# Six instead of two feature tiles of a feed-forward block in plain matrix products, and the token sums of the seven-product form as background steps

## The chip, the core and the metric

The kernel is one program on one core of a Trainium2 chip. The metric is the device time of one execution in microseconds, the median of three runs. The engines of the core are called by the short names of the profile: PE multiplies matrices, DVE and ACT work elementwise and reach both memories of the chip, POOL works elementwise on one of them, and SP issues the transfers from the chip's main memory (its queue is SPq). PEld is the loading of PE's stationary operand.

## The reference

The reference computes one transformer block with a convolution and an mLSTM branch, then two more layers with attention. Only one part of it is touched here, the first feed-forward block, where s is 512 tokens, d is 1024 and f is 2816:

```
h = rms_norm(x, norm_ffn_g[l]) * (1.0 + sc2) + sh2
gt, up = jnp.split(jnp.einsum("bsd,df->bsf", h, w_ffn_up[l]), 2, axis=-1)
x = x + g2 * jnp.einsum("bsf,fd->bsd", jax.nn.silu(gt) * up, w_ffn_down[l])
```

sc2, sh2 and g2 come from a modulation vector, `mod = silu(c) @ w_ada + b_ada`, of which each of six sections has 1024 numbers. All is float32.

## The kernel before

Tokens lie along the columns of a tile (512), features along its 128 partitions. To keep float32 accuracy every operand is split into a rounded part and a rest ("hi" and "lo": a cast on ACT, then a subtraction on DVE or POOL), and each product is three matmuls, hi·hi, hi·lo and lo·hi (`mm3`, lines 368 to 371, which therefore carry nearly all matmuls of the profile).

The weights come in half units, 128x512 numbers, with `unit` (line 342): a transfer into one of four buffers "st" (L347), the cast to "wh" on ACT (L348), the rest "wl" on DVE (L351). After each half unit, `pull` runs steps of the background list `bg`, here one step for every second half unit.

The first feed-forward block (`ffn1`, line 1118) has 22 feature tiles of 128; each stands for two column tiles of w_up, one of the gate and one of the value. They are worked on in groups of 8, 8 and 6. After each group `tmat` multiplies by the rows of w_down that belong to it: eight output tiles, each added to x with a factor of the modulation vector (`add`, L1134).

Within the first group the first two feature tiles are done by `seven_head`: four column tiles side by side, eight steps over the depth, twelve 512-column matmuls in a step, or 24 of 256 columns where the tokens' operand was split in two halves of tokens. All other feature tiles go in pairs through `seven`, a form with seven half-size products in place of eight (it multiplies the 2x2 blocks of weights and tokens; sums and differences of weight blocks are made on DVE and POOL before the product, and those of the results after it). One pair takes 14 splits (`parts`: cast L1077, rest L1078), 168 matmuls of 256 columns, six sums of weight blocks (L1099 to L1101, L1113) and seven sums of results (L1103 to L1115).

The tokens' side is made once by `seven_x` (line 986), before `seven_head`: for each of four pairs of depth tiles the normalised token tiles h1 and h2 (L1157, L1159), their own splits (L999, L1000), and two tiles of block sums, ta on DVE and tb on POOL (L1005 to L1008), with their splits. The sums serve only the products called t1 to t4 in `seven`.

Two other pieces of work are issued while `seven_head` runs: `mid` (the rest of a memory projection, L1321 and L1328, and the tables of sines and cosines for the rotary embedding, `rope_tables`, lines 556 to 585, some thirty small DVE instructions) and, as background steps, the eight steps of `ada_ops(5)`: each loads two tiles of w_ada (L599) and multiplies and sums them on DVE (L601), and gives one column of the factors that `add` of w_down needs.

The order within each engine's queue is not written by hand. A scheduler takes the instructions by their place in the program, gives out buffers, and reckons with a model of durations which instruction is ready first. Each engine runs its queue strictly in that order. Buffers of a name ("q", "pt", "hs", "t", "wh") are a fixed number, and an instruction that needs a new one waits until an old one is free.

Of the kernel before, what the change touches and what calls it, by code (L numbers as in the profile page):

```python
# [8 lines left out]
ALU = mybir.AluOpType  # L9
# [3 lines left out]
P = 128  # L13
# [10 lines left out]
UNIT = 1024  # L24
FF_GROUPS = (8, 8, 6)
FIRST = 6
LOWEST = -3.4e38
# [198 lines left out]
class Net:  # L226
# [760 lines left out]
    def seven_x(self, hs):  # L987

        nc = self.nc
        m = S // 2
        pieces = [None] * KD
        ops = {n: [] for n in ("11", "21", "22", "t1", "t2", "t3", "t4")}
        todo = []

        def split(hi, lo, src, eng=nc.vector):
            nc.scalar.copy(hi, src)  # L999
            eng.tensor_tensor(out=lo, in0=src, in1=hi.bitcast(F32), op=ALU.subtract)  # L1000

        def sums(k, h1, h2):
            ta, tb = self.t(), self.t()
            l, r = slice(0, m), slice(m, S)
            nc.vector.tensor_sub(ta[:, l], h1[:, r], h1[:, l])  # L1005
            nc.gpsimd.tensor_tensor(out=tb[:, l], in0=h2[:, r], in1=h1[:, r], op=ALU.add)
            nc.vector.tensor_add(ta[:, r], h2[:, r], ta[:, l])
            nc.gpsimd.tensor_tensor(out=tb[:, r], in0=h2[:, l], in1=ta[:, r], op=ALU.subtract)  # L1008
            ah, al = self.two("hs")
            split(ah, al, ta)  # L1010
            bh, bl = self.two("hs" if k < 2 else "pt")
            split(bh, bl, tb, nc.gpsimd)
            for n, hi, lo, c in (("t1", ah, al, l), ("t2", ah, al, r), ("t3", bh, bl, l),
                                 ("t4", bh, bl, r)):
                ops[n].append((hi[:, c], lo[:, c]))

        for k in range(KD // 2):
            h1, h2 = hs(k), hs(k + 4)
            got = []
            for i in range(2):  # L1020
                z = self.slot("q" if i else "hs", dt=F32R)
                hi, lo = z[:, 0:m], z[:, m:S]
                split(hi, lo, h1[:, i * m:(i + 1) * m])
                got.append((slice(i * m, (i + 1) * m), hi, lo))
            pieces[k] = got
            ops["11"].append(got[0][1:])
            hi, lo = self.two("hs")
            split(hi, lo, h2)
            pieces[k + 4] = [(slice(0, S), hi, lo)]
            ops["21"].append((hi[:, 0:m], lo[:, 0:m]))  # L1030
            ops["22"].append((hi[:, m:S], lo[:, m:S]))
            todo.append((k, h1, h2))
            if k:
                sums(*todo.pop(0))
        sums(*todo.pop(0))
        return pieces, ops

    def seven_head(self, name, pieces, done, mid):
# [11 lines left out]
        for n in range(4):  # L1050
            done(n, pts[n])

    def seven(self, name, tiles, x, done):
# [64 lines left out]
    def ffn1(self):  # L1118
# [36 lines left out]
        def hs(k):  # L1155
            h = self.t()
            nc.vector.scalar_tensor_tensor(out=h, in0=self.x[k], scalar=self.aff[:, 8 + k:9 + k],  # L1157
# [3 lines left out]
            return h  # L1161
        pieces, x = self.seven_x(hs)

        def mid():
            self.run_all(mem)
            self.rope_tables()
        self.bg.append(self.ada_ops(5, "q"))
        self.bg_rate = 0.5
        f0 = 0
        for n in FF_GROUPS:  # L1170
            act = []
            if not f0:
                self.seven_head("w_up", pieces, lambda t, pt: up(t, pt, act), (None, mid))
            for f in range(f0 + 2 * (f0 == 0), f0 + n, 2):
                self.seven("w_up", (f, f + 1), x, lambda *z: up2(*z, act))
            self.tmat("w_down", f0, n, KD, act, add)
            f0 += n
# [686 lines left out]
```

## Time and profile before

| | us |
|---|---|
| runs shown | 2238.39, 2234.23, 2239.53 (median 2238.39) |
| profiled execution | 2234.19, its span 2232.5 |
| PE busy | 2151.7 (96% of the span) |
| DVE busy | 1495.4 (67%) |
| ACT busy | 1045.7 (47%) |
| POOL busy | 705.7 (32%) |

Busy time of PE is modelled with overlap, so PE can be shown as busy and yet run at half its clock: the granted clock has a column of its own (PEclk, 1.00 is full). The first feed-forward block's products begin at 550.4 us in the span, its first group ends at 709.7, the second at 835 and the third at 927.

### The profile page before, as it was taken

How to read it: one execution, taken by the hardware profiler on the slowest of the kernel's cores; microseconds unless marked ns; L12 is line 12 of the kernel's file. 1: busy time of each engine (PE TensorE's matmuls, PEld its weight loads, DVE VectorE, ACT ScalarE, POOL GpSimd, SP SyncE). 2: the span in 40 equal slices, each digit the busy share in tenths (PEclk: the TensorE clock that was granted, in tenths of full speed). 3: DMA queues.
4: the chain of work that ended last, by engine and by line, in shares of the span. 5: the costliest groups of instructions: out<-in, count | busy, mean ns of one | idle time of the engine just before them, and what ended most of it. 6: DMA issues, size and time to landing. Idle time of an engine off the chain costs nothing.

```text
span 2232.5 us, 30831 instructions
## 1 busy us (share of the span) xinstructions
PE 2151.7 (96%) x10756; PEld 1776.9 (80%) x10756; DVE 1495.4 (67%) x2823; ACT 1045.7 (47%) x1971; POOL 705.7 (32%) x630
## 2 busy tenths in 40 slices
PE   6999999999789999999989999999999999999998
PEld 4887778888688989877778888888887778888886
DVE  8889989445985968759975654545556665545354
ACT  4555466645443534645464432323555645323233
POOL 3554454553462716343441210101133321101010
PEclk9999999999899999999999999999999999999999
DMA  7344443233432332321211333322321112232232
GB/s 265 111 135 133 137 132 102 76 103 103 151 95 95 95 113 82 104 76 43 71 46 64 96 95 94 94 95 94 118 86 54 32 48 90 94 95 93 94 95 88
DMA packets 120544, 217.04 MB, mean 97 GB/s; under 512 B 13762, under 2 KB 18114, under 8 KB 120388
## 3 DMA queue, kind: packets, MB, share of 16 engines
q1 hardware_dynamic: 120388, 215.08, 30.3%
q8 instruction: 84, 1.38, 0.3%
q14 instruction: 72, 0.59, 0.1%
HBM read 212.93 MB, written 2.10 MB: 96 GB/s over the span
## 4 chain that ended last, share of the span: by engine, by line
PE 74%; DVE 9%; issue 2%; ACT 1%; POOL 1%; DMA 1%; SPq 0%; DVEq 0%; ACTq 0%; POOLq 0%
PE ps L369 24%; PE ps L370 24%; PE ps L371 24%; PE ps L503 2%; DVE bias L1610 1%; DVE bias L1572 1%; DVE m L1609 1%; POOL q L1078 1%; DVE big L361 0%; DVE q L601 0%; DMA q<-in_w_up_dram 0%; DVE rope L1281 0%; DVE x L1486 0%; DVE pt L1101 0%; DVE wl L1078 0%
## 5 line engine op out<-in xcount | busy, mean ns | idle before, releaser
L348 ACT CAST wh<-st 128x512 fp32r<-128x512 f32 (+1 forms) x618 | 378.3, 616 | 671.2 <-PE ps L370 417.6
L369 PE MATMUL ps<-hs,wh 128*128 128x512 f32 (+1 forms) x1720 | 653.5, 384 | 24.9 <-ACT wh L1077 11.4
L371 PE MATMUL ps<-hs,wl 128*128 128x512 f32 (+1 forms) x1720 | 652.9, 380 | 7.5 <-DVE wl L1078 5.0
L370 PE MATMUL ps<-hs,wh 128*128 128x512 f32 (+1 forms) x1720 | 654.5, 381 | 2.5 <-DVE hs L628 2.5
L351 DVE TENSOR_TENSOR wl<-st,wh 128x512 fp32r<-128x512 f32 x408 | 298.0, 732 | 206.1 <-ACT wh L348 201.7
L369 PEld LDWEIGHTS ps<-hs,wh 128*128 128x128 f32 x1720 | 326.2, 190 | 97.6 <-ACT wh L1077 12.9
L351 POOL TENSOR_TENSOR wl<-st,wh 128x512 fp32r<-128x512 f32 (+1 forms) x210 | 285.4, 1366 | 357.6 <-ACT wh L348 328.1
L371 PEld LDWEIGHTS ps<-hs,wl 128*128 128x128 f32 x1720 | 326.1, 190 | 75.8 <-DVE wl L1078 5.6
L370 PEld LDWEIGHTS ps<-hs,wh 128*128 128x128 f32 x1720 | 326.6, 190 | 69.6 <-DVE hs L628 3.8
L1212 POOL TENSOR_TENSOR t<-t,t 128x512 f32<-128x512 f32 x44 | 69.2, 1576 | 602.7 <-DVE t L1211 533.6
L643 DVE SCALAR_TENSOR_TENSOR big<-ps,vec,big 128x511 f32<-128x511 f32 (+28 forms) x240 | 164.9, 720 | 3.5 <-ACT big L640 3.5
L370 PE MATMUL ps<-big,wh 128*128 128x512 f32 x400 | 156.9, 394 | 0.0
L369 PE MATMUL ps<-big,wh 128*128 128x512 f32 x400 | 156.1, 394 | 0.0
L371 PE MATMUL ps<-big,wl 128*128 128x512 f32 x400 | 156.1, 394 | 0.0
L361 DVE TENSOR_TENSOR big<-t,big 128x512 fp32r<-128x512 f32 (+1 forms) x106 | 74.1, 717 | 80.9 <-ACT big L360 80.6
L369 PE MATMUL ps<-wh,hs 128*128 128x512 f32 (+1 forms) x320 | 125.1, 396 | 2.9 <-ACT t L951 2.9
L370 PE MATMUL ps<-wl,hs 128*128 128x512 f32 (+1 forms) x320 | 125.9, 393 | 0.0
L371 PE MATMUL ps<-wh,hs 128*128 128x512 f32 (+1 forms) x320 | 125.1, 391 | 0.0
L451 POOL TENSOR_TENSOR t<-t,t 128x512 f32<-128x512 f32 (+1 forms) x51 | 65.8, 1290 | 173.7 <-ACT t L447 172.2
L360 ACT CAST big<-t 128x512 fp32r<-128x512 f32 (+1 forms) x106 | 53.3, 522 | 105.4 <-POOL t L1212 83.7
L369 PEld LDWEIGHTS ps<-big,wh 128*128 128x128 f32 x400 | 75.1, 188 | 17.7
L371 PEld LDWEIGHTS ps<-big,wl 128*128 128x128 f32 x400 | 75.0, 188 | 17.6
(385 smaller groups left out, 3909.4 us busy)
## 6 DMA issues: line engine op xcount, KB each, us to landing
st<-in_f_up_dram SPq DMA_DIRECT2D x176, 256.0 KB, 2.6
st<-in_f_down_dram SPq DMA_DIRECT2D x88, 256.0 KB, 2.6
st<-in_ada_dram SPq DMA_DIRECT2D x48, 256.0 KB, 2.7
st<-in_w_up_dram SPq DMA_DIRECT2D x48, 256.0 KB, 2.8
st<-in_w_down_dram SPq DMA_DIRECT2D x44, 256.0 KB, 2.6
big<-in_ada_dram SPq DMA_DIRECT2D x32, 256.0 KB, 5.1
st<-in_w_qk_dram SPq DMA_DIRECT2D x32, 256.0 KB, 2.7
st<-in_w_ogm_dram SPq DMA_DIRECT2D x32, 256.0 KB, 2.7
```

The lines of the kernel that those rows point to most:

```text
L348: nc.scalar.copy(wh, st)
L351: eng.tensor_tensor(out=wl, in0=st, in1=wh.bitcast(F32), op=ALU.subtract)
L360: nc.scalar.copy(hi, src)
L361: nc.vector.tensor_sub(lo, src, hi.bitcast(F32))
L369: nc.tensor.matmul(out, lh, rh, start=start, stop=False)
L370: nc.tensor.matmul(out, lh, rl, start=False, stop=False)
L371: nc.tensor.matmul(out, ll, rh, start=False, stop=stop)
L451: (add or nc.gpsimd).tensor_tensor(out=acc, in0=acc, in1=sq, op=ALU.add)
L503: self.nc.tensor.transpose(out, in_, self.ident[:p, :p])
L643: nc.vector.scalar_tensor_tensor(out=out[:, d:], in0=x[:, :S - d], scalar=w(j), in1=out[:, d:], op0=ALU.mult, op1=ALU.add)
L1078: eng.tensor_tensor(out=lo, in0=src, in1=hi.bitcast(F32), op=ALU.subtract)
L1212: nc.gpsimd.tensor_tensor(out=b, in0=b, in1=hold["a"], op=ALU.mult)
```

## The change

`FF_PLAIN = 6`: in the first group the feature tiles 2 to 5 no longer go through `seven` but through a new function, `seven_plain`, one column tile at a time, with the pieces of the tokens that `seven_head` uses. Only the pair 6, 7 of that group still goes through `seven`; the second and third group are as before. The sums and their splits of `seven_x` are no longer issued there but handed back as eight steps, which become the background list in place of `ada_ops(5)`; those follow as background steps from the pair 6, 7 on. The rest of tb's split is now made on DVE. The normalised tiles h1 and h2 lie in buffers "hs" and "pt" in place of "t".

```diff
+FF_PLAIN = 6
...
         def sums(k, h1, h2):
-            ta, tb = self.t(), self.t()
...
+            def one():
+                ta = hold["a"] = self.t()
+                nc.vector.tensor_sub(ta[:, l], h1[:, r], h1[:, l])
+                nc.vector.tensor_add(ta[:, r], h2[:, r], ta[:, l])
+                hi, lo = self.two("hs")
+                split(hi, lo, ta)
...
+            def two():
+                tb = self.t()
+                nc.gpsimd.tensor_tensor(out=tb[:, l], in0=h2[:, r], in1=h1[:, r], op=ALU.add)
+                nc.gpsimd.tensor_tensor(out=tb[:, r], in0=h2[:, l], in1=hold["a"][:, r],
+                                        op=ALU.subtract)
+                hi, lo = self.two("hs" if k < 2 else "pt")
+                split(hi, lo, tb)
...
+    def seven_plain(self, name, t, pieces, done):
+
+        pt = self.ps()
+        for k in range(KD):
+            if k % 4 == 0:
+                wh, wl = self.unit(name, t, k // 4)
+            c = slice(k % 4 * P, (k % 4 + 1) * P)
+            for j, (z, xh, xl) in enumerate(pieces[k]):
+                self.mm3(pt[:, z], wh[:, c], wl[:, c], xh, xl, k == 0 and j == 0, k == KD - 1)
+        done(t, pt)
...
-            h = self.t()
+            h = self.slot("hs" if k % 4 < 2 else "pt")
...
-        self.bg.append(self.ada_ops(5, "q"))
+        self.bg.append(steps)
         self.bg_rate = 0.5
...
             if not f0:
                 self.seven_head("w_up", pieces, lambda t, pt: up(t, pt, act), (None, mid))
-            for f in range(f0 + 2 * (f0 == 0), f0 + n, 2):
+                for t in range(4, 2 * FF_PLAIN):
+                    self.seven_plain("w_up", t, pieces, lambda t, pt: up(t, pt, act))
+                self.flush()
+                self.bg.append(self.ada_ops(5, "q"))
+                f = FF_PLAIN
+            for f in range(f, f0 + n, 2):
                 self.seven("w_up", (f, f + 1), x, lambda *z: up2(*z, act))
```

PE's queue has 10524 rows before and 10476 after, DVE's 2754 and 2732. After the first group the queues are the same until the first attention layer (about 1000 us in the span), where the scheduler puts the same instructions in another order; from about 1155 us on they are the same again.

DVE's queue before, just behind the last weight split of `seven_head` (L601 is an ada step, L1078 a split of the first `seven`, L1321 and L1328 the memory projection, L564 a table of angles):

```order
L601 ISA q_5589,mod<-q_5589,q_86,ada_5587 128x512
L601 ISA mod 128x1
L1078 TENSOR_TENSOR wl_5633<-pt_5620,wh_5632 128x512
L1078 TENSOR_TENSOR q_5637<-pt_5622,q_5636 128x512
L601 ISA q_5628,mod<-q_5628,q_86,ada_5626 128x512
L601 ISA mod 128x1
L1321 TENSOR_TENSOR t_5499<-t_5157,t_5493 128x256
L1321 TENSOR_TENSOR t_5504<-t_5157,t_5493 128x256
L1328 TENSOR_SCALAR t_5509<-t_5158,rmem_5491 128x256
L1328 TENSOR_SCALAR t_5517<-t_5158,rmem_5491 128x256
L564 TENSOR_SCALAR t_5529<-cst,posf 128x16 x4
L1099 TENSOR_TENSOR pt_5677<-st_5666,q_5668 128x512
```

The same place with the change (L352 is a weight split of a half unit, the L351 of before; L1345, L1352, L362 are the memory projection, L565 a table of angles):

```order
L352 TENSOR_TENSOR wl_5567<-st_5565,wh_5566 128x512
L352 TENSOR_TENSOR wl_5597<-st_5595,wh_5596 128x512
L352 TENSOR_TENSOR wl_5625<-st_5623,wh_5624 128x512
L1345 TENSOR_TENSOR t_5443<-t_5157,t_5437 128x256
L1345 TENSOR_TENSOR t_5448<-t_5157,t_5437 128x256
L1352 TENSOR_SCALAR t_5453<-t_5158,rmem_5435 128x256
L1352 TENSOR_SCALAR t_5461<-t_5158,rmem_5435 128x256
L565 TENSOR_SCALAR t_5473<-cst,posf 128x16 x2
L362 TENSOR_TENSOR big_5445<-t_5443,big_5445 128x256
L565 TENSOR_SCALAR t_5473<-cst,posf 128x16 x2
L362 TENSOR_TENSOR big_5450<-t_5448,big_5450 128x256
L362 TENSOR_TENSOR big_5456<-t_5453,big_5455 128x4x64
```

The ada steps are gone from there, and three weight splits of the plain tiles stand ahead of the memory projection and the tables.

DVE's queue before at the end of the third `seven` of the group, where w_down begins (L1111, L1114, L1115 are sums of results, L351 weight splits of w_down, L361 the splits of the new activations, L1134 the addition to x):

```order
L1111 TENSOR_TENSOR t_6222<-ps_6391,t_6222 128x512
L1078 TENSOR_TENSOR q_6817<-pt_6809,q_6816 128x512
L351 TENSOR_TENSOR wl_6562<-st_6560,wh_6561 128x512
L1114 TENSOR_TENSOR t_6273<-ps_6427,t_6273 128x512
L1115 TENSOR_TENSOR t_6308<-ps_6461,t_6308 128x512
L351 TENSOR_TENSOR wl_6582<-st_6580,wh_6581 128x512
L361 TENSOR_TENSOR big_6488<-t_6273,big_6487 128x256
L361 TENSOR_TENSOR big_6488<-t_6222,big_6487 128x256
L361 TENSOR_TENSOR big_6490<-t_6222,big_6489 128x256
L361 TENSOR_TENSOR big_6490<-t_6273,big_6489 128x256
L351 TENSOR_TENSOR wl_6600<-st_6598,wh_6599 128x512
L1134 SCALAR_TENSOR_TENSOR x_90<-ps_6503,mod,x_90 128x512
```

The same place with the change (L1132 and L1133 are the L1114 and L1115 of before, L602 an ada step, L362 the first split of the new activations):

```order
L1132 TENSOR_TENSOR t_6092<-ps_6253,t_6092 128x512
L1096 TENSOR_TENSOR q_6671<-pt_6663,q_6670 128x512
L602 ISA q_6448,mod<-q_6448,q_86,ada_6446 128x512
L602 ISA mod 128x1
L352 TENSOR_TENSOR wl_6395<-st_6393,wh_6394 128x512
L602 ISA q_6489,ada_6491<-q_6489,q_79,vec 128x512
L602 ISA ada_6491 128x1
L1133 TENSOR_TENSOR t_6127<-ps_6287,t_6127 128x512
L602 ISA q_6493,mod<-q_6493,q_86,ada_6491 128x512
L602 ISA mod 128x1
L352 TENSOR_TENSOR wl_6422<-st_6420,wh_6421 128x512
L362 TENSOR_TENSOR big_6314<-t_6092,big_6313 128x256
```

Three ada instructions with 512 columns, and two weight splits, now stand between the L1132 and the splits of the new activations, where before there was the L1115 and one weight split.

SP's queue before, while `seven_head` runs (L1066 is a load for `seven`, L599 one for an ada step):

```order
L599 DMA q_5437<-in_ada_dram 128x512
L599 DMA q_5441<-in_ada_dram 128x512
L599 DMA q_5585<-in_ada_dram 128x512
L599 DMA q_5589<-in_ada_dram 128x512
L1066 DMA st_5681<-in_w_up_dram 128x512
L599 DMA q_5624<-in_ada_dram 128x512
L1066 DMA st_5802<-in_w_up_dram 128x512
L599 DMA q_5628<-in_ada_dram 128x512
L1066 DMA pt_5620<-in_w_up_dram 128x512
L1066 DMA pt_5622<-in_w_up_dram 128x512
L1066 DMA st_5804<-in_w_up_dram 128x512
```

With the change, at the end of the plain tiles (L348 is a half unit, L1084 a load for `seven`, L600 one for an ada step):

```order
L348 DMA st_5911<-in_w_up_dram 128x512
L348 DMA st_5941<-in_w_up_dram 128x512
L1084 DMA pt_6016<-in_w_up_dram 128x512
L1084 DMA pt_6018<-in_w_up_dram 128x512
L348 DMA st_5962<-in_w_up_dram 128x512
L1084 DMA q_6064<-in_w_up_dram 128x512
L600 DMA q_6066<-in_ada_dram 128x512
L600 DMA q_6070<-in_ada_dram 128x512
L1084 DMA q_6079<-in_w_up_dram 128x512
L348 DMA st_5992<-in_w_up_dram 128x512
L600 DMA q_6081<-in_ada_dram 128x512
L1084 DMA st_6062<-in_w_up_dram 128x512
```

The ada loads have moved behind the half units of the plain tiles, and stand between the loads of the pair 6, 7.

## Rows read from the trace of the kernel before

**Rows 1.** The page's 40 slices of 55.8 us, busy tenths.
```profile
PE   6999999999789999999989999999999999999998
DVE  8889989445985968759975654545556665545354
```

**Rows 2.** Stages: length, busy us of PE PEld DVE ACT POOL, PEclk, DMA, GB/s.
```profile
550.40:578.30 27.90, 25.76 (x150) 22.77 (x151) 27.87 (x48) 16.60 (x33) 16.68 (x16) 0.94 0.47 153
578.30:666.00 87.70, 67.65 (x509) 65.65 (x508) 77.69 (x141) 38.93 (x76) 44.93 (x28) 0.88 0.32 103
666.00:709.70 43.70, 43.70 (x190) 35.43 (x190) 23.05 (x35) 13.01 (x24) 6.51 (x5) 1.00 0.31 102
709.70:790.40 80.70, 79.50 (x674) 79.08 (x673) 70.77 (x86) 39.01 (x75) 53.99 (x35) 1.00 0.31 98
790.40:835.00 44.60, 44.60 (x194) 36.00 (x193) 25.55 (x38) 14.32 (x26) 6.67 (x5) 1.00 0.35 106
1000.00:1150.00 150.00, 134.02 (x705) 106.91 (x704) 140.33 (x379) 83.78 (x194) 54.42 (x67) 0.97 0.17 52
```

**Rows 3.** Waits of PE, 550 to 666 us: total us, times, longest.
```profile
PE ps L369 <- ACT wh L1077: 10.7, 3, 8.2
PE ps L371 <- DVE wl L1078: 5.0, 3, 1.7
PE ps L369 <- ACT t L1125: 4.3, 1, 4.3
PE ps L493 <- DVE t L490: 1.4, 1, 1.4
PE ps L371 <- DVE wl L351: 0.7, 1, 0.7
```

**Rows 4.** PE's timeline: start, length, line, operation.
```profile
553.42 0.41 PE L369 MATMUL ps<-q,wh 128*128 128x256 f32 x1
...
555.13 0.37 PE L371 MATMUL ps<-q,wl 128*128 128x256 f32 x1
555.33 0.39 PE L369 MATMUL ps<-hs,wh 128*128 128x512 f32 x1
...
558.13 0.28 PE L369 MATMUL ps<-hs,wh 128*128 128x256 f32 x1
...
560.93 0.39 PE L369 MATMUL ps<-hs,wh 128*128 128x512 f32 x1
...
709.71 0.28 PE L369 MATMUL ps<-hs,wh 128*128 128x256 f32 x1
...
722.67 0.28 PE L371 MATMUL ps<-hs,q 128*128 128x256 f32 x1
```

**Rows 5.** DVE's timeline in the first seven.
```profile
583.34 0.68 DVE L1099 TENSOR_TENSOR pt<-st,q 128x512 f32<-128x512 f32 x1
583.95 0.74 DVE L601 CUSTOM_DVE_ANT_0 q<-q,q,vec 128x512 f32<-128x512 f32 x1
...
590.13 0.68 DVE L1101 TENSOR_TENSOR pt<-pt,pt 128x512 f32<-128x512 f32 x1
...
612.88 0.68 DVE L1111 TENSOR_TENSOR t<-ps,t 128x512 f32<-128x512 f32 x1
613.48 0.68 DVE L1078 TENSOR_TENSOR q<-pt,q 128x512 fp32r<-128x512 f32 x1
```

**Rows 6.** ACT's timeline in the first seven.
```profile
590.85 0.62 ACT L1077 CAST wh<-pt 128x512 fp32r<-128x512 f32 x1 [7.45 <-DVE pt L1101]
```

**Rows 7.** DVE by line, 578 to 666 us: busy us, mean ns.
```profile
L1101 DVE TENSOR_TENSOR pt<-pt,pt 128x512 f32<-128x512 f32 x6 | 7.7, 1313 | 0.0
L601 DVE CUSTOM_DVE_ANT_0 q<-q,q,ada 128x512 f32<-128x512 f32 x6 | 4.5, 742 | 0.0
L601 DVE CUSTOM_DVE_ANT_0 q<-q,q,vec 128x512 f32<-128x512 f32 x4 | 3.0, 745 | 1.3 <-DMA q<-in_ada_dram 1.3
L1078 DVE TENSOR_TENSOR q<-st,q 128x512 fp32r<-128x512 f32 x3 | 2.0, 680 | 0.0
```

More of the change, by code (lines that the diff above doesn't have):

```diff
@@ L995, in seven_x @@
         ops = {n: [] for n in ("11", "21", "22", "t1", "t2", "t3", "t4")}
-        todo = []
+        steps = []
+        l, r = slice(0, m), slice(m, S)
         def split(hi, lo, src, eng=nc.vector):
@@ L1002, in sums @@
         def sums(k, h1, h2):
-            ta, tb = self.t(), self.t()
[L1004 to L1015, printed above, removed]
+            hold = {}
+            def one():
[4 more added lines that the diff above has]
+                split(hi, lo, ta)
+                ops["t1"].append((hi[:, l], lo[:, l]))
+                ops["t2"].append((hi[:, r], lo[:, r]))
+            def two():
[5 more added lines that the diff above has]
+                split(hi, lo, tb)
+                ops["t3"].append((hi[:, l], lo[:, l]))
+                ops["t4"].append((hi[:, r], lo[:, r]))
+            return [one, two]
         for k in range(KD // 2):
@@ L1019, in seven_x @@
             got = []
-            for i in range(2):
+            for i, c in enumerate((l, r)):
                 z = self.slot("q" if i else "hs", dt=F32R)
                 hi, lo = z[:, 0:m], z[:, m:S]
-                split(hi, lo, h1[:, i * m:(i + 1) * m])
-                got.append((slice(i * m, (i + 1) * m), hi, lo))
+                split(hi, lo, h1[:, c])
+                got.append((c, hi, lo))
             pieces[k] = got
@@ L1029, in seven_x @@
             pieces[k + 4] = [(slice(0, S), hi, lo)]
[L1030 to L1036, printed above, removed]
+            ops["21"].append((hi[:, l], lo[:, l]))
+            ops["22"].append((hi[:, r], lo[:, r]))
+            steps += sums(k, h1, h2)
+        return pieces, ops, steps
     def seven_head(self, name, pieces, done, mid):
@@ L1161, in hs @@
             return h
-        pieces, x = self.seven_x(hs)
+        pieces, x, steps = self.seven_x(hs)
         def mid():
@@ L1171, in ffn1 @@
             act = []
+            f = f0
             if not f0:
                 self.seven_head("w_up", pieces, lambda t, pt: up(t, pt, act), (None, mid))
-            for f in range(f0 + 2 * (f0 == 0), f0 + n, 2):
+                for t in range(4, 2 * FF_PLAIN):
[4 more added lines that the diff above has]
+            for f in range(f, f0 + n, 2):
                 self.seven("w_up", (f, f + 1), x, lambda *z: up2(*z, act))
```

## The prediction, made before the change was run

> **What bounds the kernel now.** I read the page's slices first [rows 1]: PE is busy nearly everywhere, and the eleventh and twelfth slice (558 to 670 us) are the only ones near the first feed-forward block that show a 7 and an 8, with DVE at 9 and 8. So I cut that block into stages [rows 2]. The reader is to compare two rows: three `seven` pairs take 87.7 us in the first group (578.3 to 666.0), four pairs take 80.7 in the second (709.7 to 790.4). It is the same code; 29.2 us a pair against 20.2.
>
> What a pair costs when nothing waits comes from PE's timeline [rows 4]: 110 matmuls of 256 columns from 709.71 to 722.67 are 0.1178 us each, 168 are 19.8 us. The second group's four pairs are 79.2 of 80.7: PE sets the pace, and all waits cost 1.5. In the first group 59.4 of 87.7 is work, and 28.3 is not. PE's waits name 20.0 of it [rows 3]: 10.7 for the cast L1077, 5.0 for the rest L1078, 4.3 for `up`'s Silu. The other 8.3 is the clock: PE counts as busy for 67.65 us where it has 59.4 us of work, at a granted clock of 0.88 in the mean, since it runs at half speed after each long wait, as it does at 553 us (0.214 us a matmul of 256 columns) behind the wait for the first token tile.
>
> Who causes the longest wait, 8.2 us, is seen in DVE's queue. The load of the block of weights arrives, L1099 is done at 583.34, an ada step stands next, then memory projection and rope; L1101, which needs only L1099 and POOL's reading, starts at 590.13 [rows 5], and ACT, idle for 7.45 us, casts its result at 590.85 [rows 6]. The 4.3 us is alike: ACT's Silu stands behind the sine, and that behind DVE's angles. DVE is busy for 77.7 of 87.7 us in this stage and for 27.87 of 27.90 in the head [rows 2]. So the stage is bound by DVE's in-order queue, into which five things fall at once: token sums, ada steps, rope, memory projection and the weight work of the sevens.
>
> **The change, part by part.** All sums are made against the profiled execution, 2234.2 us (span 2232.5), the first group being 27.9 + 87.7 + 43.7 = 159.3 us of it.
>
> *The plain tiles.* Eight column tiles, each with four depth tiles as 24 matmuls of 256 columns and four as 12 of 512. Both forms stand in the head: 12 of 512 from 555.33 to 558.13 and 24 of 256 from there to 560.93, 2.80 us each [rows 4]. A column tile is 5.60, eight are 44.8. They replace two pairs, 39.6: PE gets 5.2 us more work. That is the price.
>
> *What they ask of DVE.* The stretch from the first plain weight split to the last split of new activations holds, by the order, 45 instructions of 512 columns, 12 of 256, 4 ada products and 34 small ones. Back to back the 512s start every 0.60 us (612.88, 613.48 [rows 5]): 27. The 256s at about half of their 0.68 [rows 7] are 4, the ada products at 0.745 are 3; the small ones at half a split's 0.68 would be 12, at a tenth 2. That is 36 to 46 us beside 44.8 of PE. But 13 of the 512s (7.8 us) belong to the pair 6, 7 and aren't due yet, so 28 to 38 is due, and I take the plain tiles at PE's pace. Their weights run four buffers ahead, 11.2 us of PE's work, which covers the memory projection and rope in DVE's queue. If the cover fails, the nearest wait is the 0.7 for L351 in the head [rows 3]: 16 half units times 0.7 would be 11. Bounds 0 and +11; I take 0, nearest to the head, where seven of eight steps wait for no weights.
>
> *The head.* Its eight steps are 22.4. The first keeps its half clock, 20 matmuls at 0.097 more, 1.9, and 0.4 is the broadcast of the memory projection. DVE loses two of four ta sums there and most ada steps; the broadcast's operand (L490) stands earlier in DVE's queue, so the wait of 1.4 goes. 24.7 against 27.9. Bounds 24.3 and 27.9 (nothing gained); I take 24.7, since DVE, full before, is the one relieved.
>
> *The pair that stays.* 19.8 plus the second group's 1.5 for its waits, 21.3. It begins as that group's first does, its front part made ahead. Lower bound 19.8, upper bound the mean of the three before, 29.2, if all of its trouble comes along.
>
> *The ada steps.* Eight steps of two products, at 0.742 and 0.745 [rows 7], 11.9 us of DVE. By the order one step stays in the head, two are made at the end of the plain tiles, one in the pair and four where w_down begins. Ahead of w_down DVE has 23.05 of 43.70 us to do [rows 2], so 6 fit. What queues behind them is L1132, L1133 and the splits of the last two activations; PE has 18 + 18 + 3 matmuls of w_down's first three tiles to do before it needs those, 9 us at 0.233. At most three products delay that chain, 2.2 us. Cost 0; it is +2 if the 9 us are used up by the chain itself. On SP their loads have moved past the half units of the plain tiles, and now stand among the loads of the pair and of w_down; one that waits for a free "q" buffer holds those behind it. I take 0, as the half units ahead are loaded early; a late one would be a wait within the pair, whose bounds hold it.
>
> *tb's rests on DVE.* Four splits at 0.60, 2.4 us, in the stretch counted above. The h tiles in "hs" and "pt" wait for nothing that isn't free by then: 0.
>
> *w_down.* The second group's 44.6 [rows 2], as against 43.7, of which three matmuls lay in the stage before.
>
> *Attention.* From about 1000 to 1150 us the scheduler orders the same instructions otherwise. PE is idle for 16 of 150 us there and DVE busy for 140 [rows 2]. No instruction is added, so I take 0, and bound it by half of that idle time, 8 us either way.
>
> Sum: 24.7 + 44.8 + 21.3 + 44.6 = 135.4, 23.9 us below 159.3. The profiled execution would be 2210.3. It lies 4.2 below the median of 2238.39; the same 23.9 below the median gives **2214.5**.
>
> **A rule weighed.** DVE's L1101 takes 1313 ns in the mean where an equally large L1078 takes 680 [rows 7]; the long ones lie beside POOL's instructions. The Trainium skill, page "SBUF — State Buffer", section "SBUF: two separate sides", says that DVE instructions with two SBUF inputs and POOL share a port pair that one of them holds for its whole instruction, while the other fully blocks. By that rule taken as a plain sum, DVE and POOL times would add up, and a pair would be paced by both: this would make the pair beside the ada steps the next jam. The second group's row speaks against the sum: 70.77 of DVE and 53.99 of POOL lie in 80.7 us with PE waiting 1.2 [rows 2], so the durations shown already hold the blocking. By the row it costs nothing more; by the sum it is the first rival below.
>
> **The rivals.** *The pair that stays inherits the jam.* DVE's 70.77 / 4 = 17.7 us of a pair, with four ada steps (5.9) and POOL's 13.5 against it, are 37.1 us for 21.3 + 9 of cover: 6.8 us of wait, and half clock after it. At its bound of 29.2 the pair costs 7.9 more: 2222.4. For it speaks that the first group's pairs waited behind ada steps; against it, that rope and sums are done by then. *The new order in attention costs*: 8 us, 2222.5; or gives 8, 2206.5. For it speaks that DVE is the bound there, so the order decides when PE is fed; against it, that the work is equal. *The other side: the plain tiles are fed too late.* A half unit passes SP, ACT and DVE, one after the other, and in-order queues on both hold memory projection, rope and Silu between. If each of 16 half units waited as the L1078 did at its longest, 1.7 us [rows 3], this is 27 us: 2242, slower than before. It decides from 1.5 us a half unit on (23.9 / 16). Against it stand the four buffers and DVE's 28 to 38 us. *The change doesn't do what it says:* sums of the first two depth pairs stand within the head by the order anyway, so the head may keep its 27.9: 2217.7.
>
> **How the numbers follow.** Forecast 0.70 (own range 2209 to 2220, the head that keeps its 27.9 included); jam in the pair 0.11; attention's order by 5 us or more, either way, 0.10; plain tiles fed too late 0.05, of which 0.04 slower than before; no difference for a reason not seen here 0.04. The range is 2206 to 2227: attention's gain at its low end, pair and a part of the attention's loss at the high end, 2214.5 + 7.9 + 4.6. About 0.3% (6.7 us) is what a measurement of this kernel can tell from no change: faster 0.91, within it 0.05, slower 0.04.
>
> **What would show it.** Right: the three `seven` pairs' stage is replaced by eight plain tiles of 5.6 us with a granted clock of 1.00 and no wait over 1 us; one pair of about 21; L1119 (the L1101 of before) done while PE still works on plain tiles; first group about 135 us. Wrong: half clock within the plain tiles, waits of PE for L351's or L348's successors there (plain tiles fed late), waits for POOL's or DVE's rests in the pair 6, 7 (jam), or a first group of 135 us and a stage from 975 us on that has changed by more than 5.

## The result, and the profile after

The median is 2212.27 us (four runs, 2210.00 to 2217.06) against 2238.36 us before (four runs beside them): a ratio of 0.989, 95% interval 0.987 to 0.991, or 26.1 us less. 2214.5 was predicted. The profiled execution took 2214.43 us (span 2212.4).

The page's slices of the kernel after (40 slices of 55.3 us, busy tenths), which answer to [rows 1]:

```profile
PE   6999999999999999998999999999999999999998
DVE  8889889454876959859975644535546665445354
```

The 7 and the 8 of PE in the eleventh and twelfth slice are gone. The stages, in the columns of [rows 2]: head, plain tiles, the pair 6, 7, w_down, the second group's pairs:

```profile
556.48:581.58 25.10, 25.10 (x151) 22.81 (x151) 20.75 (x45) 15.46 (x33) 2.59 (x6) 0.93 0.29 85
581.58:627.02 45.44, 45.44 (x290) 41.05 (x288) 34.12 (x84) 21.42 (x39) 13.50 (x8) 1.00 0.39 123
627.02:646.80 19.78, 19.78 (x169) 19.78 (x168) 13.88 (x24) 8.44 (x16) 8.57 (x6) 1.00 0.52 159
646.80:694.60 47.80, 44.96 (x194) 35.83 (x193) 31.99 (x54) 15.11 (x27) 7.32 (x5) 1.00 0.44 139
694.60:775.10 80.50, 79.65 (x674) 79.30 (x673) 70.69 (x86) 39.16 (x75) 53.84 (x35) 1.00 0.31 100
```

The first group takes 25.1 + 45.4 + 19.8 + 47.8 = 138.1 us instead of 159.3. PE's waits from 556 to 695 us, in the form of [rows 3], are two lines, and the second stands for the normalised token tile that the head begins with:

```profile
PE ps L372 <- DVE wl L352: 2.8, 2, 1.9
PE ps L370 <- ACT hs L1001: 2.5, 1, 2.5
```

Nothing is left of the 20.0 us of [rows 3] in plain tiles and pair, nor of the half clock: the granted clock is 1.00 from the first plain tile on. The 2.8 us are new, and lie in w_down.

The whole account, profiled execution against profiled execution: first group -21.2, second and third group -0.8 (217.6 to 216.8), from there to the end -4.2 (1305.2 to 1301.0). That is -26.2, close to the 26.1 of the medians. Ahead of the block this execution lost 6.1 us (head at 556.5 instead of 550.4), so the two spans are only 20.1 us apart. The instructions there are the same in the same order; 5.8 of the 6.1 us arise between 307 and 318 us, in waits of 2.85 us for a cast on ACT (L361) and 1.14 us for its rest on DVE (L362) and in the half clock behind them (granted clock 0.74 in that stretch, 1.00 before):

```profile
311.02 0.50 PE L370 MATMUL ps<-q,q 128*128 128x512 f32 x1 [2.85 <-ACT q L361]
```

Eleven of the twelve kernels below, also the same up to the block, begin it at 549.9 to 552.5, so this is a difference of executions, not of the kernel.

### The profile page after: what moved, and what is told of

It reads as the page before. It is cut to its first block, busy times and chain, and to the rows that moved or that the text cites. A ratio compares the mean times of both kernels' runs of the same rounds, so it can differ in the third digit from the quotient of the medians.

```text
span 2212.4 us, 30653 instructions
## 1 busy us (share of the span) xinstructions
PE 2151.1 (97%) x10708; PEld 1774.0 (80%) x10708; DVE 1470.8 (66%) x2801; ACT 1036.3 (47%) x1953; POOL 670.3 (30%) x606
## 4 chain that ended last, share of the span: by engine, by line
PE 77%; DVE 5%; issue 1%; ACT 1%; POOL 1%; DMA 0%; SPq 0%; ACTq 0%; POOLq 0%; DVEq 0%
PE ps L370 25%; PE ps L371 25%; PE ps L372 25%; PE ps L504 2%; DVE bias L1634 1%; DVE m L1633 1%; DVE bias L1596 0%; DVE x L1510 0%; DVE rope L1305 0%; PE ps L465 0%; DMA q<-in_ada_dram 0%; POOL q L1096 0%; PE ps L494 0%; DVE pt L362 0%; POOL wl L1096 0%
## 5 line engine op out<-in xcount | busy, mean ns | idle before, releaser
L349 ACT CAST wh<-st 128x512 fp32r<-128x512 f32 (+1 forms) x634 | 388.0, 616 | 689.9 <-PE ps L371 429.8
L372 PE MATMUL ps<-hs,wl 128*128 128x512 f32 (+1 forms) x1736 | 659.7, 381 | 1.7 <-POOL wl L1096 1.7
L352 DVE TENSOR_TENSOR wl<-st,wh 128x512 fp32r<-128x512 f32 x424 | 307.9, 728 | 206.5 <-ACT wh L349 204.6
L352 POOL TENSOR_TENSOR wl<-st,wh 128x512 fp32r<-128x512 f32 (+1 forms) x210 | 287.5, 1376 | 352.0 <-ACT wh L349 328.8
L362 DVE TENSOR_TENSOR big<-t,big 128x512 fp32r<-128x512 f32 (+1 forms) x102 | 72.6, 728 | 80.9 <-ACT big L361 80.5
L361 ACT CAST big<-t 128x512 fp32r<-128x512 f32 (+1 forms) x102 | 52.9, 535 | 105.3 <-POOL t L1236 83.6
L372 PEld LDWEIGHTS ps<-big,wl 128*128 128x128 f32 x400 | 75.1, 188 | 21.2 <-DVE wl L352 3.7
```

What stands on the lines that cost most here:

```text
L349: nc.scalar.copy(wh, st)
L352: eng.tensor_tensor(out=wl, in0=st, in1=wh.bitcast(F32), op=ALU.subtract)
L362: nc.vector.tensor_sub(lo, src, hi.bitcast(F32))
L372: nc.tensor.matmul(out, ll, rh, start=False, stop=stop)
```

## The experiments

All stage times are read from one profile each, to about 0.1 us and in the same way: head from its first matmul, pairs to the first closed run of w_down's matmuls, w_down to its last. "Lead" is the time at which PE is through with what stands ahead of the first pair (the head, or the plain tiles), less the start of the pair's first finished block sum on DVE (L1101 before, L1119 after): 5.4 us with the change (627.02 - 621.64), and -11.8 before (578.3 - 590.13, [rows 2, 5]). With the change:

```profile
621.64 0.69 DVE L1119 TENSOR_TENSOR pt<-pt,pt 128x512 f32<-128x512 f32 x1 [1.19 <-POOL st L1118]
```

A negative lead means that PE is ready for the pair before the pair's second product has operands. In three kernels (steps alone, ada late, both late) the pair's first weights are late too, and its first matmul comes 15.1, 3.0 and 1.9 us behind that point.

| kernel | lead | head | plain | pairs | w_down | first group | median | ratio to before, 95% |
|---|---|---|---|---|---|---|---|---|
| before | -11.8 | 27.9 | - | 87.7 (3) | 43.7 | 159.3 | 2238.4 | 1 |
| after | 5.4 | 25.1 | 45.4 | 19.8 (1) | 47.8 | 138.1 | 2212.3 | 0.987 to 0.991 |
| plain tiles alone | 9.6 | 30.5 | 44.8 | 19.1 (1) | 44.4 | 138.8 | 2214.1 | 0.987 to 0.991 |
| steps alone | -20.5 | 26.1 | - | 100.2 (3) | 43.8 | 170.0 | 2249.9 | 1.003 to 1.006 |
| tables late | -11.4 | 28.1 | - | 79.4 (3) | 45.9 | 153.4 | 2230.1 | 0.995 to 0.998 |
| ada late | -9.5 | 25.1 | - | 88.0 (3) | 42.1 | 155.3 | 2234.7 | 0.997 to 0.999 |
| both late | -8.2 | 25.1 | - | 84.6 (3) | 45.5 | 155.2 | 2233.2 | 0.996 to 0.999 |
| pair first | -6.8 | 30.4 | 45.4 | 33.3 (1) | 44.5 | 153.6 | 2227.0 | 0.994 to 0.997 |
| four plain | -5.1 | 26.1 | 22.7 | 56.0 (2) | 44.5 | 149.4 | 2225.9 | 0.992 to 0.995 |
| four plain, tables late | -5.1 | 25.1 | 22.7 | 57.1 (2) | 44.8 | 149.7 | 2227.9 | 0.994 to 0.997 |
| the same, last product late | -1.5 | 25.1 | 22.7 | 54.4 (2) | 43.0 | 145.2 | 2226.1 | 0.993 to 0.996 |
| four plain, tables late, ada early | -2.1 | 26.0 | 22.7 | 45.4 (2) | 44.4 | 138.6 | 2219.8 | 0.990 to 0.994 |
| ada early | 6.4 | 25.1 | 45.4 | 19.8 (1) | 44.4 | 134.7 | 2208.4 | 0.985 to 0.989 |
| eight plain | none | 26.0 | 68.2 | - | 44.5 | 138.6 | 2216.3 | 0.988 to 0.991 |

### The two halves of the change

Plain tiles alone (the sums at once, the ada steps from the head on):

```diff
-            steps += sums(k, h1, h2)
+            steps.append(sums(k, h1, h2))
+            if k:
+                for f in steps.pop(0):
+                    f()
+        for f in steps.pop(0):
+            f()
...
-        self.bg.append(steps)
+        self.bg.append(self.ada_ops(5, "q"))
...
-                self.flush()
-                self.bg.append(self.ada_ops(5, "q"))
```

> The kernel after, with its eight plain column tiles, but the token sums made at once as in the kernel before, and the eight ada steps as background steps from the head on. First theory (the queue): the three pairs were slow because DVE's in-order queue held too much at that place, and the plain tiles make the room; the sums then fit almost anywhere. Head back to at most 27.9 us (25.1 with the change), plain tiles 44.8 to 47, pair 19.8 to 21, w_down 44.6 (no ada steps left in it): first group 138 to 141 us (138.1 with the change), time 2212 to 2216 us. Second theory (the steps): it is the deferred sums that relieve DVE; with sums and ada steps at the front again, half of the gain goes: first group about 150 us, time about 2224 us.

Measured: 138.8 us, 2214.1 us. Its stages:

```profile
550.80:581.26 30.46, 27.20 (x150) 24.30 (x151) 30.46 (x61) 17.71 (x35) 11.60 (x12) 0.89 0.56 167
581.26:626.08 44.82, 44.82 (x289) 40.38 (x288) 34.82 (x91) 21.75 (x41) 4.20 (x3) 1.00 0.43 129
626.08:645.13 19.05, 19.05 (x169) 19.05 (x168) 11.74 (x16) 8.89 (x15) 7.41 (x6) 1.00 0.42 126
645.13:689.57 44.44, 44.44 (x194) 36.04 (x193) 23.78 (x36) 12.80 (x23) 5.65 (x5) 1.00 0.32 96
```

The first theory holds in its sum: the plain tiles carry the gain. Within it, DVE is busy in all of the head's 30.46 us, which loses 5.4 us. It is also longer than the 27.9 of the kernel before and of the expectation. A reason that no run tests by itself: DVE makes the rests of tb's split there, as with the change, four instructions of 0.68 us that POOL made before. And w_down, without ada steps, is 3.4 us shorter than with the change.

Steps alone:

```diff
-FF_PLAIN = 6
+FF_PLAIN = 2
```

> The kernel after with FF_PLAIN = 2: the sums are background steps and the ada steps come after the head, but three pairs go through seven in the first group as before. First theory (the queue): memory projection, tables and the rest of the sums, some 27 us of DVE work, stand in one piece between the last weight split of the head and the first block sum of the first pair; PE waits there once for 12 to 15 us and runs at half clock behind it, and then pairs take 20 us each. Head 25, pairs 77, w_down 45 to 47, first group about 148 us, time about 2227 us. Second theory (the steps): the moved sums and ada steps are the gain; pairs 60 to 63 us, first group 132 to 135, time 2207 to 2212 us. Third theory (only plain tiles heal the place, since seven is slow there by itself): pairs 85 or more, time 2233 us or more.

Measured: 170.0 us and 2249.9 us, 11 us slower than before. The first wait came as the first theory said, 15.1 us; the pairs behind it did not recover, and took 100 where it had 77. The numbers are those of the third theory. But seven is not slow there by itself: behind four plain tiles, with the ada steps out of the way, two pairs take 45.4 us (below). So deferring sums and ada steps without plain tiles does harm. PE's waits from 575 to 680 us, and where DVE's queue stood (start, length, line; in brackets the idle time ahead and its releaser):

```profile
PE ps L370 <- ACT wh L1095: 25.3, 4, 15.1
PE ps L372 <- DVE wl L1096: 4.7, 4, 1.6
```

```profile
568.67 0.68 DVE L352 TENSOR_TENSOR wl<-st,wh 128x512 fp32r<-128x512 f32 x1
576.27 0.76 DVE L1345 TENSOR_TENSOR t<-t,t 128x256 f32<-128x256 f32 x2 [6.93 <-ACT t L499]
...
596.13 0.68 DVE L1117 TENSOR_TENSOR pt<-st,q 128x512 f32<-128x512 f32 x1
...
599.09 0.68 DVE L1119 TENSOR_TENSOR pt<-pt,pt 128x512 f32<-128x512 f32 x1
```

DVE did nothing for 6.93 us: the memory projection's first product stood at the head of its queue and waited for the broadcast that PE makes at the end of the head. The remaining sums stood behind it, though ACT had made their tokens by 561.2. They also hold a buffer: those tokens lie in "pt", into which the pair's first weights are loaded, and SP's queue waited until the sums (L1009, at 587.5) had read them:

```profile
SPq L1084 <- DVE t L1009: 18.8, 2, 18.2
```

The load was issued at 588.0, and PE's 15.1 us ended at 593.7. With the change three weight splits of the plain tiles stand ahead of that product.

### Less work for DVE, without plain tiles

Three kernels move work away in the kernel before: the tables, the ada steps, and both. The tables leave the first group. The ada steps leave the head and the first two pairs, but not the three pairs as a whole: 11 of their 16 products start between 632.9 us, where the third pair begins, and the end of the pairs; in the kernel before 9 started within the three pairs.

```diff
             self.run_all(mem)
-            self.rope_tables()
...
+            if f0 == 8:
+                self.rope_tables()
```

```diff
-        self.bg.append(self.ada_ops(5, "q"))
...
             for f in range(f0 + 2 * (f0 == 0), f0 + n, 2):
+                if f == 6:
+                    self.bg.append(self.ada_ops(5, "q"))
```

> The kernel before with one thing moved: the tables of sines and cosines (11.6 us of DVE in thirty small instructions) are issued at the start of the second group of feature tiles instead of in the head. First theory (the queue): the wait of 8.2 us in the first pair falls to 3 or less and the one of 4.3 us for the Silu behind the sine goes, with the half clock behind them: first group 144 to 148 us instead of 159.3, time 2224 to 2228 us; the second group, where DVE has room, stays within 1 us. Second theory (only the sums matter) and third (seven is slow at that place by itself): first group 155 or more, time 2234 us or more.

> The kernel before with one thing moved: the eight ada steps (some 13 us of DVE and sixteen loads) are issued from the pair 6, 7 on instead of from the head on; three pairs, sums and tables as before. First theory (the queue): the first pair's block sum stands ahead of the tables then, waits of the three pairs fall from 20 us to 6 or so and the half clock with them; w_down takes 2 to 3 us more for the ada steps, as with the change: first group 140 to 146 us, time 2219 to 2225 us. Third theory (seven is slow at that place by itself): first group 155 or more, time 2234 us or more.

> The kernel before with both moved: ada steps from the pair 6, 7 on and the tables of sines at the start of the second group; three pairs, sums as before. Alone, the tables gave 5.9 us of the first group (159.3 to 153.4) and the ada steps 4.0 (to 155.3). First theory (the queue, by its load): DVE has some 53 us left for 61 us of PE in the three pairs, so the waits vanish; pairs 62 to 68 us, head 28, w_down 46 to 50 as both now fall there: first group 137 to 145 us, time 2216 to 2224 us. Rival (the gains of single moves only add up, since each wait that goes uncovers the next one): first group about 149 us, time 2228 us.

Measured: 5.9, 4.0 and 4.1 us off the first group. All three are faster than before by their intervals, and all three expectations of the first theory were far too large; "both" did not even add up, as its rival expected. The late ada steps lie in the range of the third theory; 2.8 of their 4.0 us are the head's, and the pairs took 88.0 us, as before. The theory of the load falls with the tables, which are gone from the group. The block sum still starts at 589.94, where it started at 590.13 before, since other work moved up into the room, and PE's longest wait is 7.9 us, 8.2 before:

```profile
PE ps L369 <- ACT wh L1077: 9.5, 2, 7.9
```

With both late DVE is shown as busy for 74.85 of 84.60 us, though it has 109 instructions there instead of 141 [rows 2]:

```profile
575.00:659.60 84.60, 68.81 (x511) 65.65 (x512) 74.85 (x109) 37.25 (x72) 46.04 (x32) 0.90 0.38 124
```

What all three have in common with the kernel before is a lead of -8 us or less (among them its size does not give the time of the pairs: 79.4 us at -11.4, 88.0 at -9.5). That gave the second theory: not how much DVE has to do, but how far ahead of the pair its front part (load, block sums, cast, rest) is made. The second group's first pair has a lead of 9.6 us (709.71 - 700.07), built up while PE works on w_down, and its four pairs wait for 1.2 us.

### The same work in another order

The pair right behind the head, the eight plain tiles behind it (against the run with plain tiles alone):

```diff
                 self.seven_head("w_up", pieces, lambda t, pt: up(t, pt, act), (None, mid))
-                for t in range(4, 2 * FF_PLAIN):
+                self.seven("w_up", (2, 3), x, lambda *z: up2(*z, act))
+                for t in range(8, 16):
...
-                f = FF_PLAIN
+                f = 8
```

> The kernel of the run with plain tiles alone (its first group took 138.8 us), with the same pieces in another order: the one pair through seven comes right after the head, as feature tiles 2 and 3, and the eight plain column tiles behind it. The same instructions of DVE and PE stand in the group. Theory of the load (what counts is how much DVE has to do in the group): about 139 us again, time about 2214 us. Theory of the lead (what counts is how far ahead of the pair's first matmul its first block sum is made; it was 5.4 us ahead with the change, 9.6 ahead with plain tiles alone, 11.8 us behind in the kernel before): the block sum comes 10 us or more behind the pair's start, the pair takes 32 to 38 us instead of 19, head 29 to 31, plain tiles 44.8, w_down 44.5: first group 151 to 158 us, time 2226 to 2233 us.

Measured: 153.6 us, 2227.0 us; the pair took 33.3 us with a lead of -6.8 (the expectation had -10 or less). Its stages (head, pair, plain tiles):

```profile
550.00:580.40 30.40, 27.73 (x150) 25.09 (x151) 30.40 (x62) 16.76 (x35) 11.52 (x12) 0.85 0.50 154
580.40:613.68 33.28, 24.80 (x168) 24.06 (x167) 32.05 (x79) 16.12 (x32) 10.80 (x8) 0.79 0.35 109
613.68:659.12 45.44, 45.44 (x291) 41.08 (x291) 19.95 (x29) 15.69 (x29) 3.95 (x3) 1.00 0.35 107
```

PE has the same matmuls as in the run with plain tiles alone, DVE 170 instructions in these three stages against 168 there, and the head is as long; 14.8 us come from the order. The reader is to see the granted clock of 0.79: of the pair's 13.5 us too much, 8.5 are named waits, and 5.0 the half clock behind them.

### Fewer plain tiles: what sets the lead

```diff
-FF_PLAIN = 6
+FF_PLAIN = 4
```

> The kernel after with FF_PLAIN = 4: four plain column tiles and two pairs, 2.6 us less PE work. First theory (the queue, by its load): memory projection, tables and all sums are some 50 us of DVE up to the first block sum, for 47.5 us of head and plain tiles, so the first pair starts 3 to 7 us late and the rest of it at half clock: first group 138 to 146 us, time 2212 to 2220 us. Rival (four tiles are room enough): 135.5 us, time 2209 us. From the end of the third group on the order is that of the kernel after: 1301 us.

Measured: 149.4 us and 2225.9 us, lead -5.1. The lead is that of the first theory, 3 to 7 us late; the group and the time are longer than it allows (146 and 2220 us), and the load is not the cause, as the next two runs show. The same with the tables in the second group (the edit above):

> The run with FF_PLAIN = 4 (first group 149.4 us; its first pair's block sum was made 5.1 us behind the pair's start), with the tables of sines (11.6 us of DVE) moved to the second group. The ada steps stay in the two pairs. Theory of the lead: the block sum now comes 2 to 7 us ahead of the pair's start; the first pair takes 20 us and the second 20 to 24, since four ada steps in the first pair eat some 4 us of the lead: head 26, plain 22.4, pairs 40 to 44, w_down 46 to 47: first group 135 to 140 us, time 2209 to 2215 us. If the ada steps in the pairs were what jammed them, the waits of 3.6 and 5.7 us stay: 146 us or more, time 2221 us or more.

Measured: 149.7 us. The 11.6 us taken away moved the lead by nothing, -5.1 again, and the expectation of 135 to 140 was wrong; the rival's 146 or more came out, with waits of 3.6 and 5.3 us in the pairs. DVE's timeline shows why:

```profile
603.67 0.69 DVE L1147 TENSOR_TENSOR t<-ps,t 128x512 f32<-128x512 f32 x1 [3.19 <-PE ps L372]
...
605.66 0.69 DVE L1117 TENSOR_TENSOR pt<-st,q 128x512 f32<-128x512 f32 x1
...
608.60 0.68 DVE L1119 TENSOR_TENSOR pt<-pt,pt 128x512 f32<-128x512 f32 x1
```

DVE idles for 3.19 us with L1147 at the head of its queue, the product of the last plain tile, which can't start before PE has finished that tile. The pair's block sum stands behind it, so by this reading the order fixes the lead, whatever DVE had to do earlier. Issuing that one product later:

```diff
             dve.tensor_sub(a[i], a[i], s[i])
+        while self.later:
+            self.later.pop(0)()
...
-        done(t, pt)
+        if t == 2 * FF_PLAIN - 1:
+            self.later.append(lambda: done(t, pt))
+        else:
+            done(t, pt)
```

> The run with FF_PLAIN = 4 and late tables once more; there DVE stood idle for 3.2 us ahead of the first pair, with the product of the last plain tile at the head of its queue, which waits for PE's last matmul of that tile, and the pair's split, block sum and an ada step behind it (block sum L1119 5.1 us behind the pair's start, first group 149.7 us). Here that one product is issued behind the pair's block sums in the program, and the scheduler puts a split, the first half of the block sum and one ada product ahead of it; no other work is added or taken away. If the order in the queue sets the lead (head of the line, not the amount of work): the block sum comes 1 to 3 us behind the pair's start, and the first group is 144 to 147 us. If something else holds the block sum (its loads, POOL, the ada steps): it stays 4 to 5 us behind and the first group at 149 to 150 us. The time changes by 3 us at most, to 2224 to 2228 us; the reading is that of the stage.

Measured: lead -1.5, first group 145.2, both as expected; the first pair's wait for the cast of its block sums fell from 3.6 to 1.8 us. (Line numbers are higher by 6 here: L1121 and L1123 are the block sums, L1153 the product.)

```profile
596.42 0.68 DVE L1121 TENSOR_TENSOR pt<-st,q 128x512 f32<-128x512 f32 x1
...
599.09 0.69 DVE L1153 TENSOR_TENSOR t<-ps,t 128x512 f32<-128x512 f32 x1 [1.32 <-PE ps L373]
...
600.36 0.69 DVE L1123 TENSOR_TENSOR pt<-pt,pt 128x512 f32<-128x512 f32 x1
```

A wait of 5.3 us for the second pair's cast stayed in both. Its cause is the ada steps in the first pair, by the next run, which puts them ahead of the pairs (diff of the ada steps below, tables late, `bg_rate` 0.67):

> FF_PLAIN = 4, tables of sines in the second group, and the ada steps right behind the sums in the background list (rate 0.67 instead of 0.5, so that all sixteen steps fall into head and plain tiles). DVE then has some 50 us of work due ahead of the first block sum for 48 us of head and plain tiles. By the theory of the lead it is on the edge: if the block sum comes out ahead of the pair's start, both pairs run at 20 us each and w_down at 44.5: first group 132 to 134 us, the lowest of all, time 2206 to 2208 us; if it comes 2 to 5 us behind, the pairs lose 5 to 10 us: 138 to 143 us, time 2212 to 2217 us. I take the second.

Measured: lead -2.1, pairs 45.4 us for two instead of 57.1, 138.6 us: the case that was chosen. PE waits for 1.6, 0.65 and 0.86 us there. Its time, 2219.8 us, is 3 above that range: the second group and the stage from the third on took 1.5 and 2.7 us more than in the kernel before. Why the second group is 1.5 to 3.4 us longer in the four kernels with four plain tiles stays open.

### The ada steps where w_down begins

```diff
-        self.bg.append(steps)
+        self.bg.append(steps + self.ada_ops(5, "q"))
...
                 self.flush()
-                self.bg.append(self.ada_ops(5, "q"))
```

> The kernel after with the eight ada steps right behind the sums in the background list, so that they fall into the plain tiles and none is left where w_down begins. If the 3 us that w_down takes too long (47.8 against 44.6) are the ada steps ahead of its weight splits: head 25, plain tiles 45, pair 19 to 20, w_down 44.5, first group 134 to 135 us instead of 138.1, time 2208 to 2210 us. Rival (DVE is full in the plain tiles: 34.1 us and 12 more of 45): PE waits there for weight splits, plain tiles 48 to 50 us, first group 137 to 140, time 2211 to 2216 us. From the end of the third group on the order is that of the kernel after, so this stage should take its 1301.0 us and not the 1305.2 of the kernel before.

Measured: 25.1 + 45.4 + 19.8 + 44.4 = 134.7 us, and PE waits for nothing from the first plain tile to the end of w_down. Head, plain tiles, pair and w_down:

```profile
551.77:576.86 25.09, 25.09 (x151) 22.79 (x151) 25.05 (x57) 14.14 (x30) 2.58 (x6) 0.93 0.62 195
576.86:622.30 45.44, 45.44 (x290) 41.05 (x288) 38.91 (x94) 25.00 (x47) 13.12 (x9) 1.00 0.39 127
622.30:642.09 19.79, 19.79 (x170) 19.79 (x169) 13.02 (x17) 8.62 (x15) 8.23 (x7) 1.00 0.43 134
642.09:686.53 44.44, 44.44 (x195) 36.04 (x193) 23.70 (x36) 12.80 (x23) 5.42 (x5) 1.00 0.30 96
```

So the ada steps were the 3.4 us of w_down. Their room is not where the expectation put it: 13 of the 16 products start in the head, in which DVE is now busy for 25.05 of 25.09 us without PE being late, and only three in the plain tiles. At 2208.4 us this is the lowest of all versions. Its interval overlaps with that of the kernel after; that it beats it rests on the stage, not on the total.

With all eight tiles plain, on top of this:

```diff
-FF_PLAIN = 6
+FF_PLAIN = 8
```

> FF_PLAIN = 8: no pair in the first group, twelve plain column tiles, and the ada steps behind the sums in the background list as in the run with early ada steps. Against that run the last pair's 19.8 us become four column tiles, 22.4: first group 2.6 us longer if the pair has no waits left, 136 to 138 us. The order from the third group on is that of the kernel before, so I expect 1305 us there: time about 2214 us. If the pair still cost more than its work (22 us or more), this version would be equal or shorter in the first group, 134 to 135.5 us.

Measured: 138.6 us and 2216.3 us, 3.9 us of the group more than with early ada steps: 22.7 for four column tiles instead of 19.8 for the pair, and 0.9 in the head. A pair with a lead costs its work and no more, so the plain form is dearer wherever the lead exists. The time from the third group on was 1309.6 us, not the 1305 expected.

## Why the prediction was right

The number was right, and so were the terms that carry it. Two terms taken as zero were not, +3.2 us where w_down begins and -4.2 in attention, and nearly cancelled: that the total came within 2.3 us is partly luck.

- *The head*, 24.7: 25.1. That DVE was the one relieved is shown by the run with plain tiles alone: sums and ada steps at the front give DVE 30.46 of 30.46 us and a head of 30.5. Moving either was enough: with the sums at the front and only the ada steps moved (ada late) the head is 25.1 too, and so it is with most ada steps in it and the sums as steps (ada early).

```profile
550.31:575.42 25.11, 25.11 (x150) 22.47 (x150) 23.35 (x35) 15.07 (x30) 14.61 (x12) 0.93 0.18 52
```

- *The plain tiles*, 44.8, never fed late: 45.4, no wait, granted clock 1.00. DVE was busy for 34.1 us, within the 28 to 38 said to be due. A tile took 5.68 us instead of 5.60; the rival of late weights has nothing for it.
- *The pair that stays*, 21.3: 19.8, its lower bound. The reason given, that its front part is made ahead, is the one that the experiments single out: L1119 at 621.64 while PE is in the plain tiles until 627.02. The plain sum of the rule that was weighed does not pace it: DVE's 13.88 and POOL's 8.57 us lie in 19.78.
- *The ada steps*, 0 (or +2): this is the step that failed. w_down took 47.8, 3.2 more than the 44.6 forecast. The prediction looked at the splits of the last activations behind them; what came late were w_down's own weight splits. DVE also stood idle for the ada loads, which the step on SP's queue had as a possible wait in the pair. Both are in DVE's timeline of the kernel after:

```profile
646.11 0.75 DVE L602 CUSTOM_DVE_ANT_0 q<-q,q,ada 128x512 f32<-128x512 f32 x1 [0.92 <-DMA q<-in_ada_dram]
...
650.90 0.75 DVE L602 CUSTOM_DVE_ANT_0 q<-q,q,vec 128x512 f32<-128x512 f32 x1 [1.49 <-DMA q<-in_ada_dram]
...
656.41 0.74 DVE L602 CUSTOM_DVE_ANT_0 q<-q,q,ada 128x512 f32<-128x512 f32 x1
...
657.08 1.74 DVE L352 TENSOR_TENSOR wl<-st,wh 128x512 fp32r<-128x512 f32 x1
```

PE's longer wait ends with that L352:

```profile
658.87 0.50 PE L372 MATMUL ps<-big,wl 128*128 128x512 f32 x1 [1.94 <-DVE wl L352]
```

DVE was idle for 0.92 and 1.49 us and made ada products ahead of each weight split, and the two splits that PE waited for took 1.77 and 1.74 us instead of 0.68, beside POOL (last section): 2.8 us of wait.

- *Attention*, 0 with a bound of 8: -4.2. The order decided, as the rival said, though by less than its 8. The place is 1101.7 to 1133.7 us before and 1087.4 to 1114.9 after, 115 matmuls each, all but two of them the same:

```profile
1101.70:1133.70 32.00, 25.04 (x115) 20.19 (x114) 30.81 (x105) 17.96 (x46) 15.08 (x22) 0.89 0.16 53
```

```profile
1087.40:1114.90 27.50, 24.62 (x115) 20.32 (x114) 27.10 (x98) 16.68 (x42) 14.72 (x22) 0.88 0.19 62
```

PE's longest wait in the first, for DVE's L1652, has no counterpart after, where no wait is over 0.84 us:

```profile
1125.75 0.80 PE L369 MATMUL ps<-big,q 128*128 128x512 f32 x1 [2.09 <-DVE mx L1652]
```

The experiments repeat it without having been made for it. From w_down's end in the third group to the end of the program, three kernels whose queues are there in the order of the kernel after (it, ada early, pair first) took 1301.0, 1301.9 and 1302.9 us; three in the order of the kernel before (it, tables late, eight plain) 1305.2, 1305.9 and 1309.6. The others' order is neither's in some part of that stretch. But POOL's queue has one of the two orders there in all fourteen kernels: the five with that of the kernel after took 1298.4 to 1303.6 us, the nine with that of the kernel before 1304.4 to 1309.6. So the order decides, by some 5 us in the mean; kernels of one order lie up to 5.2 us apart, and the exact 4.2 is that of two executions.

- *The cause of the jam*, "five things fall at once into DVE's in-order queue": the queue is right, "at once" is not enough. Moving 11.6 us of the five (the tables), 13 (the ada steps) or both to a later place gave 4 to 6 us; the same instructions in another order cost 14.8; one product issued later gave 4.5. The plain tiles help because DVE keeps up with PE there (34.1 of 45.4 us, with sums and tables in it), and because the pair's front part stands ahead of what must wait for PE. The prediction's reading of the 8.2 us counts a little too much to the queue: 583.34 is the start of L1099, not its end, and POOL's reading, which L1101 waits for as well, ended at 585.81. The 4.3 us from there to 590.13 are the queue's.

```profile
584.11 1.70 POOL L1100 TENSOR_TENSOR st<-st,pt 128x512 f32<-128x512 f32 x1 [8.83 <-DMA q<-in_ada_dram]
```

## What to carry to other kernels

Before a form with a long chain (load, sums, cast, rest, product), read how far ahead of its first matmul the last operand is made, in one row of the timeline for each engine: with a lead it cost its own matmuls here, 19.8 us, without one up to 33. To build a lead, put plain work ahead of it, and look in the in-order queue for an instruction that waits for PE and stands ahead of the chain; taking 11.6 us of load off the engine did not help here while that instruction stood there. Look also at the buffers that the chain's loads need: deferred work may hold them. And count what a deferred background step delays at its new place: here it was the next stage's weight splits.

## What was not expected of the hardware

DVE's busy time is not its load. Beside POOL's instructions the same DVE instruction is shown as longer. In the pairs of the run with both late 21 of DVE's 109 instructions took over 0.9 us, each of them beside one of POOL's; with the tables (11.6 us) gone from there the busy time is only 2.8 us shorter than before. Two block sums of 0.68 us each are shown there as 3.46 together, while POOL's L1100 and L1142 run (DVE, then POOL):

```profile
606.62 3.46 DVE L1101 TENSOR_TENSOR pt<-pt,pt 128x512 f32<-128x512 f32 x2 [0.58 <-POOL st L1100]
```

```profile
604.94 2.89 POOL L1100 TENSOR_TENSOR st<-st,pt 128x512 f32<-128x512 f32 x2 [3.44 <-issue]
607.79 1.74 POOL L1142 TENSOR_TENSOR t<-t,t 128x512 f32<-128x512 f32 x1
```

The Trainium skill, page "SBUF — State Buffer", section "SBUF: two separate sides", has DVE instructions with two SBUF inputs and POOL instructions hold one port pair in turn, each for its whole length; these rows agree with it. In the kernel after DVE's weight splits of w_down are hit too, 1.77 and 1.74 us at 653.45 and 657.08.

One thing stays open: the pair's 168 matmuls took 19.05 us with plain tiles alone and 19.78 with the change, both without a wait at a granted clock of 1.00, and a plain tile 5.60 and 5.68.
